# SSM output tables a quarter early, a third table buffer, regrouped gate matmuls and split z tiles in a hybrid FoX/S5/ConvFFN block

## The chip, the cores and the metric

The kernel runs on one core of one Trainium2 chip. The metric is the time of one execution in device microseconds (us); lower is better. Each kernel's time is the median of several runs. The engines are named as the profile names them: PE (TensorE, matrix multiply), DVE (VectorE), ACT (ScalarE), POOL (GpSimd) and SP (SyncE, which only issues DMAs here).

## The reference

One layer of a hybrid encoder block on 1024 tokens of width 1024, with 16 learned meta tokens put in front (1040 positions in all). The part that the change touches is the mixer:

```
xn   = rmsnorm(h)
q, k, v, f_logit, u, gates = split(xn @ w_in)        # 8 heads x 64; u: 512; gates: 2 x 1024
y_a  = forgetting_attention(q, k, v, f_logit) @ w_attn_out
z    = gelu(s5(u))            # 32 groups x 16 channels, 64 complex states per group
zg   = z @ w_glu
y_s  = zg[:, :1024] * sigmoid(zg[:, 1024:])
g    = sigmoid(gates)
h    = h + (g[:, :1024] * y_a + g[:, 1024:] * y_s) @ w_o
```

Behind it come a gated feed-forward block with a causal convolution of width 3, another residual, and a final norm. Nothing there is touched. All values are float32.

## The kernel before, in words

Each float32 operand is split into a high and a low part of 128x128 blocks (`whi`/`wlo` for weights, `xhi`/`xlo` for the normed input), and each product is three matmuls: hi·hi, hi·lo, lo·hi (L159 to L161, called dense below). One gate chunk is 128 gate channels over 1026 columns: three column blocks of 342 (`QBLK`), eight blocks of the depth, three matmuls each, so 72 dense matmuls. There are 16 gate chunks. The eight for the SSM half (i = 8 to 15) and one of the attention half (`AHEAD = 1`, i = 0) run in the gate stage, beside the SSM. The rest run later, as filler between the scores and products of attention (`GA = [1, 1, 1, 3]` chunks per pair of heads).

The program before the feed-forward part goes: load, norm and split of x (to about 60 us) together with the product for u; the gate stage with the SSM (about 60 to 200 us); forget gate, q and k of the first pair of heads; the product of z with `w_glu` (`seven`, L221 to L223, a form with seven half-size products; from 235 us); then attention (first scores, L748 and L749, at 383 us).

The SSM works in chunks of eight positions and in four quarters of eight groups each. Per quarter q:
- input table: DVE makes `Vm`, PE transposes it, ACT copies it to `Wi` (L1756);
- chain, first part: PE multiplies `Wi` with `U`, ACT copies `wr`, `wi` (L1771, L1772);
- output table (`output_tables`): DVE makes `Gm` (products into `Gm` and `tm`, then a difference), PE multiplies it with the input matrix, ACT copies that into `Kt` (L1733), DVE adds a diagonal to `Kt` (16x128), and eight DMAs on SP lay `Kt` out as a block Toeplitz matrix `Tm` (L1741);
- chain, second part: DVE rotates `wr`, `wi` (with cosines and sines made by `rotation`, one for quarters 0 and 1, one for 2 and 3), scans along the chunks, and writes the states `St`;
- chain, third part: PE sums `Gm`·`St` (L1811) and `Tm`·`U` (L1813) into `Y`, ACT copies (L1814) and applies gelu (L1815), a DMA stores `Y` to `y_d`.

`Gm` and `Tm` have two buffers each, `St` and `Y` share three. Before the change the third part of quarter q stands right behind the output table of quarter q, and `rotation(1)` stands inside the second part of quarter 2.

The order on each engine isn't written out: instructions are recorded in a program order, and a scheduler orders each engine's queue by it and by data. On its engine each instruction is then run in that order, and a waiting instruction holds up all behind it. Tiles live in pools; a tile on memory that another held waits until the other's last use. Attention's filler is a generator (`stream`) from which `fill` draws an equal share at each of 28 hooks in a pair.

For z, `load_z` reads `y_d` back into four tiles `zt`, casts them to hi (ACT, L586) and lo (DVE, L129) in `zhi`/`zlo` of four blocks, and forms the differences `zf` (L596 to L599) that become z1, z2, z3 and the block T4 (ACT cast L603, DVE lo L129). The weights' sums and parts are the tiles `ops` (L616).

Of the kernel before, what the change touches and what calls it, by code (L numbers as in the profile page):

```python
# [9 lines left out]
F = mybir.dt.float32  # L10
# [9 lines left out]
P = 128  # L20
# [30 lines left out]
def block_kernel(ctx, tc, x, meta, xbt, x0t, g1t, w_q, w_k, w_v, w_f, w_u, w_g, b_f, w_ao, lam_d, bw_d, cw_d,  # L51
# [7 lines left out]
    def pool(stack, name, bufs=1, side=None, **k):  # L59
        return stack.enter_context(  # L60
            tc.tile_pool(name=name, bufs=bufs, side=side, reuse_waits="tile", **k))
# [216 lines left out]
    xlo = xp.tile([P, KD, L], R, name="xlo")  # L278
    st_s = ExitStack()
    sp = pool(st_s, "ssm", side="left")  # L280
    st_n = ExitStack()
    n1 = pool(st_n, "norm1", side="left")

# [6 lines left out]
    g1T = n1.tile([P, KD], F, name="g1T")  # L290
    S.dma_start(g1T, g1t)
    GP.dma_start(xm, meta)
    ssm_log, ssm_loads, ssm_steps = ssm(tc, after, sp, st_ps, ident, u_d, y_d, lam_d, bw_d, cw_d, d_sk, l_dt)
    queue = []

    def load(dst, src):
# [2 lines left out]
        if len(queue) > 1:  # L299
            after(*queue[:-3:-1])  # L300

    FIRST = [(0, 1), (1, 1), (2, 2), (4, 2), (6, 2)]
    for k, n in FIRST:
        load(xT[0][k // 4][:, k % 4:k % 4 + n], x0t[:, k:k + n])
        load(uraw[k // 2][:, k % 2:k % 2 + n], w_u[:, k:k + n])
# [7 lines left out]

    def load_x(i):
        tag, bufs = ("Gm", 2) if i in (5, 6) else ("sy", 3)
        place[i] = sp.tile([P, D], F, tag=tag, name="xt", bufs=bufs)
        load(place[i], x[P * (i - 1):P * i])

    load_block(1, "Wi")
    for i in range(5, 9):  # L320
        load_x(i)
    us2, ul2 = (sp.tile([P, 2, n, SW if n == 2 else NCH], dt, tag="pc", name=nm, bufs=2)
                for n, dt, nm in ((CH, F, "usb"), (2, R, "ul")))
    ul = [sp.tile([P, 2, SW], R, tag="U", name="ul", bufs=2) for _ in range(2)] + [ul2[:, i] for i in range(2)]


    st_u = ExitStack()
# [85 lines left out]
    for b in (2, 3):  # L413
        last = normed_features(b)
        if b == 2:
            gate0 = [sp.tile([P, KD, P], dt, tag=tag, name="g0", bufs=n)
                     for dt, tag, n in ((F, "Tm", 2), (R, "sy", 3), (R, "Tm", 2))]
            GP.dma_start(gate0[0], w_g[KD])
            S.copy(gate0[1], gate0[0])
            lo_by_dma(gate0[2], gate0[1], w_g[KD])  # L420
        else:
            late.append(last)
        if b == 3:
            for q in (0, 1):
                factors(q)
            for q in (0, 1):
                normed_features(q)
        for m in range(4):
            ps = u_product(b, m)
            S.copy(us_part(b, m), by_chunks(ps[:, :UBLK[b][1]]))  # L430
# [18 lines left out]
        chains[q] = ssm_chain(q)  # L449
        next(chains[q])  # L450

    begin(0)
    ssm_out(0)
    begin(1)
    for q in range(4):
        next(chains[q])
        if q:
            ssm_out(q)
        run(chains[q])
        if q < 2:  # L460
            begin(q + 2)
    st_u.close()
    st_n.close()


    st_f = ExitStack()
    fp = pool(st_f, "fgate", side="right")
    fraw = fp.tile([P, KD, H], F, name="fraw")
# [8 lines left out]
    gp_ = pool(st_g, "gates", side="right")  # L477

    okeep = {}
    AHEAD = 1  # L480

    def gate_chunk(i, pl, tanh):
        whi, wlo = gate0[1:] if i == KD else wchunk(w_g[i], KD, GP, act=not tanh)
        if tanh:
            gs = pl.tile([P, LQ], F, tag="gs", name="gs", bufs=1)
        for t, n in QBLK:
            ps = mm_ps()
            yield from dense_steps(ps[:, :n], whi, wlo, xhi[:, :, T0 + t:T0 + t + n],
                                   xlo[:, :, T0 + t:T0 + t + n], KD)
            if tanh:  # L490
                S.activation(gs[:, t:t + n], ps[:, :n], AF.Tanh, scale=0.5)
            else:
                gs = pl.tile([P, LQ // 3], F, tag="gs", name="gs", bufs=2)
                S.activation(gs, ps[:, :n], AF.Sigmoid)  # L494
                GP.dma_start(g_d[P * i:P * i + P, t:t + n], gs)
        if tanh:
            GP.tensor_scalar(gs, gs, 0.5, 0.5, ALU.mult, ALU.add)
            if pl is not gp_ and i == KD - 1:
                okeep["g"] = gs
            else:  # L500
                SY.dma_start(g_d[P * i:P * i + P], gs)

    for i in [*range(KD, 2 * KD), *range(AHEAD)]:
        run(gate_chunk(i, gp_, False))
    st_g.close()
    st_s.close()

# [54 lines left out]
    TH = L // 2  # L562
    NC2 = NCH // 2
    T3, T2, T1 = ([zp.tile([P, 2, TH], R, name=f"z{i}{w}") for w in "hl"] for i in (3, 2, 1))
    zhi = zp.tile([P, 4, L], R, name="zhi")
    zlo = zp.tile([P, 4, L], R, name="zlo")

    def zblock(r, h_):
        return [t_[:, 2 * r:2 * r + 2, TH * h_:TH * h_ + TH] for t_ in (zhi, zlo)]

    def fold(t_):
        return t_.rearrange("p (n j) -> p j n", j=CH)
# [1 line left out]
    def load_z():  # L574
        zts = []
        for m in range(4):
            tag = "gl" if m % 2 else "ms"
            zt = gz.tile([P, CH, NCH], F, tag=tag, name="zt", bufs=2)
            ym = y_d[m].rearrange("(j c) g n -> g c j n", c=GC)
            for g in range(GQ):  # L580
                (GP if m == 3 and g % 2 else SY).dma_start(zt[GC * g:GC * g + GC], ym[g])
            zts.append(zt)
        for m in range(4):
            w_ = NC2 if m < 2 else NCH
            zh, zl = (fold(t_[:, m, :CH * w_]) for t_ in (zhi, zlo))
            S.copy(zh, zts[m][:, :, :w_])  # L586
            split_lo(V, zl, zts[m][:, :, :w_], zh)

        def part(r, h_, k):
            return zts[2 * r + k][:, :, NC2 * h_:NC2 * h_ + NC2]  # L590

        T4 = zblock(0, 1)
        for k in range(2):
            fa, fb = (gz.tile([P, L], F, tag="cg", name="zf", bufs=2) for _ in range(2))
            f1, f2, f3, f4 = (fold(f_[:, TH * q:TH * q + TH]) for f_ in (fa, fb) for q in range(2))
            V.tensor_tensor(f1, part(0, 1, k), part(0, 0, k), ALU.subtract)  # L596
            GP.tensor_tensor(f3, part(1, 1, k), part(0, 1, k), ALU.subtract)
            V.tensor_tensor(f2, part(1, 1, k), f1, ALU.subtract)
            V.tensor_tensor(f4, part(1, 0, k), f2, ALU.subtract)  # L599
            for f_, t_ in zip((fa, fa, fb, fb), (T1, T2, T3, T4)):  # L600
                q = 0 if t_ is T1 or t_ is T3 else TH
                hi, lo = t_[0][:, k], t_[1][:, k]
                S.copy(hi, f_[:, q:q + TH])  # L603
                split_lo(V, lo, f_[:, q:q + TH], hi)
        return T4

    def glu(i):
# [208 lines left out]
        S.copy(ot[:, :w], po[64:, :w])  # L816
        V.tensor_tensor(ob[64 * e:64 * e + 64, :w], po[:64, :w], ot[:, :w], ALU.add)

    GA = [1, 1, 1, 3]
    SLACK = 5  # L820
    QKN = 2 * len(BLK) * 3 * KD
    GAN = len(QBLK) * 3 * KD
# [33 lines left out]

    units = [((0,), e) for e in range(2)] + [((c, c + 1), e) for c in range(1, len(TILES), 2) for e in range(2)]
    mm_n[1] = False
    done = AHEAD
    for pr in range(H // 2):  # L860
        fbs = []
        for e in range(2):
# [614 lines left out]
        room[0] += len(groups[g])  # L1477


def ssm(tc, after, sp, s_ps, ident, u_d, y_d, lam_d, bw_d, cw_d, d_sk, l_dt):  # L1480
    nc = tc.nc
    V, S, GP, PE, SY = nc.vector, nc.scalar, nc.gpsimd, nc.tensor, nc.sync
    n_small = [0]
# [13 lines left out]
    bufs = dict(Gm=2, Tm=2, Wi=2, U=2, tq=3, sy=3, wr=2, wi=2, dt8=1, ta=1, tb=1, pc=2, dg=1)  # L1497

    def big(tag, shape, name=None):
        return sp.tile(shape, F, tag=tag, name=name or tag, bufs=bufs[tag])  # L1500

    def sm(shape, name=None, dt=F):
        n_small[0] += 1
# [16 lines left out]
    def rest():  # L1520
# [194 lines left out]

            return g0, bcx, bcp

        def output_tables(qt):
            g0, bcx, bcp = views(qt)
            Gm = big("Gm", [P, GQ, CH + 1, GC])  # L1720
            tm = big("tq", [P, GQ, CH + 1, GC], "tm")
            TT(Gm, bcx(cA, CH + 1), bcp(pr, CH + 1), ALU.mult)
            TT(tm, bcx(cB, CH + 1), bcp(pi, CH + 1), ALU.mult)
# [35 lines left out]
        def chain(qt):  # L1759
# [14 lines left out]
            dt8 = big("dt8", [P, HQ, NCH])  # L1774
            S.copy(dt8, dec[:, qt * HQ:qt * HQ + HQ].unsqueeze(2).broadcast_to([P, HQ, NCH]))
            GP.memset(dt8[:, :, 0:1], 0.0)
            if qt == 2:
                rot.append(rotation(1))
            rc, rs = (t_[:, qt % 2 * HQ:qt % 2 * HQ + HQ] for t_ in rot[qt // 2])
            ta, tb = (big(n, [P, HQ, NCH]) for n in ("ta", "tb"))  # L1780
            TT(ta, wr, rc, ALU.mult)
# [34 lines left out]
            GP.dma_start(y_d[qt], Y)  # L1816

        yield input_tables, output_tables, chain

    return log, loads, rest()  # L1820

# [57 lines left out]
```

## Time and profile before

| | |
|---|---|
| time, three runs | 1483.76, 1485.49, 1488.69 us; median 1485.49 us |
| profiled execution | 1486.44 us, span 1484.7 us |
| PE busy | 1440.5 us, 97% of the span |
| DVE, ACT, POOL busy | 73%, 49%, 51% of the span |
| busy PE per 50 us, 150 to 200 us | 46.50 us |
| busy PE per 50 us, 200 to 250 us | 44.07 us |
| busy PE per 50 us, 350 to 400 us | 47.78 us |

The rows of the page give busy time, the share of the span and the number of instructions per engine. A timeline row gives start, duration, engine, line, operation, tiles and sizes; in square brackets stands how long the engine had been idle before it and what it waited for. A windows row gives, for one stretch, its length and the busy time of PE, of PE's weight loads, of DVE, ACT and POOL, then the TensorE clock that was granted (1.00 is full speed), the DMA share and GB/s. Matmuls overlap, so a matmul's duration is longer than its step to the next.

### The profile page before, as it was taken

The page shows a single profiled execution, that of the slowest core. Times are in us where ns is not written, and L with a number is a line of the kernel's source. Part 1 is how long each engine was busy: PE and PEld are TensorE (multiplying, and loading weights), DVE is VectorE, ACT ScalarE, POOL GpSimd, SP SyncE. Part 2 cuts the span into 40 slices and gives each one's busy share as a digit, 9 for nine tenths or more (in the row PEclk, how much of TensorE's full clock was granted, in tenths as well). Part 3 has the DMA queues.
Part 4 walks back from the last instruction along what each step waited for, and adds up shares of the span by engine and source line. Part 5 has one row for each costly group of instructions (what it writes and reads, how often), then busy time and mean ns, then how long its engine had stood idle before and what let it go on. Part 6 is the DMA issues. An engine that isn't in the chain of part 4 may idle for free. (4 is left out here: it accounts for less than half of the span.)

```text
span 1484.7 us, 26535 instructions
## 1 busy us (share of the span) xinstructions
PE 1440.5 (97%) x9646; PEld 1357.2 (91%) x9646; DVE 1079.2 (73%) x2197; ACT 725.6 (49%) x1420; POOL 759.0 (51%) x890
## 2 busy tenths in 40 slices
PE   8999998999999999999999999999999999998997
PEld 7999987998899999999889999999999999777786
DVE  6987929882566676656468977888887766788685
ACT  7545547541465565542645534444434445553433
POOL 1632224752446556513862144555544327789766
PEclk9999998999899999999999999999999999999999
DMA  7665481451117342156974145677653214866413
GB/s 281 188 163 135 128 158 59 158 170 43 41 58 192 94 97 94 37 173 223 267 176 151 58 134 130 176 187 198 173 140 109 80 59 170 293 205 157 140 50 114
DMA packets 89558, 209.85 MB, mean 141 GB/s; under 512 B 14458, under 2 KB 22026, under 8 KB 89044
## 3 DMA queue, kind: packets, MB, share of 16 engines
q1 hardware_dynamic: 69492, 161.50, 32.7%
q0 software_dynamic: 18208, 42.98, 15.0%
q10 hardware_dynamic: 1728, 3.68, 0.7%
q8 instruction: 76, 1.25, 0.3%
q14 instruction: 54, 0.44, 0.1%
HBM read 169.04 MB, written 69.35 MB: 161 GB/s over the span
## 5 line engine op out<-in xcount | busy, mean ns | idle before, releaser
L159 PE MATMUL mm<-xhi,whi 128*128 128x342 f32 (+2 forms) x480 | 157.0, 327 | 0.0
L161 PE MATMUL mm<-xhi,wlo 128*128 128x342 f32 (+2 forms) x480 | 156.6, 326 | 0.0
L160 PE MATMUL mm<-xlo,whi 128*128 128x342 f32 (+2 forms) x480 | 155.6, 325 | 0.0
L1114 POOL TENSOR_TENSOR ov<-ov,og 128x1024 f32<-128x1024 f32 x21 | 51.1, 2435 | 123.4 <-ACT og L1113 119.5
L129 DVE TENSOR_TENSOR sw<-sf,sw 128x512 fp32r<-128x512 f32 x72 | 70.3, 977 | 51.6 <-ACT sw L1105 51.3
L1105 ACT CAST sw<-sf 128x512 fp32r<-128x512 f32 x72 | 45.0, 625 | 106.7 <-POOL sf L1231 74.5
L160 PEld LDWEIGHTS mm<-xlo,whi 128*128 128x128 f32 x480 | 91.1, 190 | 0.6 <-issue 0.4
L159 PEld LDWEIGHTS mm<-xhi,whi 128*128 128x128 f32 x480 | 91.1, 190 | 0.5 <-ACT gs L494 0.2
L161 PEld LDWEIGHTS mm<-xhi,wlo 128*128 128x128 f32 x480 | 91.0, 189 | 0.5 <-issue 0.2
L798 ACT CAST th<-tp 128x256 fp32r<-128x256 f32 (+3 forms) x120 | 56.2, 472 | 63.0 <-PE tp L791 32.1
L1231 POOL TENSOR_TENSOR sf<-raw,sf 128x512 f32<-128x512 f32 x36 | 61.4, 1704 | 44.0 <-DVE sw L129 43.9
L129 DVE TENSOR_TENSOR tl<-tp,th 128x256 fp32r<-128x256 f32 (+3 forms) x120 | 65.2, 546 | 25.0 <-ACT th L798 23.8
L1231 POOL TENSOR_TENSOR sf<-raw 128x512 f32<-128x512 f32 x36 | 47.8, 1328 | 68.9 <-DMA raw<-in_w_up_dram 39.1
L223 PE MATMUL mm<-xhi,sw 128*128 128x258 f32 (+1 forms) x288 | 81.0, 281 | 0.0
L221 PE MATMUL mm<-xhi,sw 128*128 128x258 f32 (+1 forms) x288 | 80.8, 281 | 0.0
L222 PE MATMUL mm<-xlo,sw 128*128 128x258 f32 (+1 forms) x288 | 80.7, 280 | 0.0
L763 POOL TENSOR_SCALAR pt<-pt,nm 128x144 f32<-128x144 f32 (+4 forms) x72 | 52.3, 738 | 51.0 <-DVE nm L762 50.5
L1283 DVE SCALAR_TENSOR_TENSOR ov<-hv,cwt,ov 128x1024 f32<-128x1024 f32 x36 | 73.9, 2054 | 0.2 <-ACT ov L1281 0.2
L1105 ACT CAST sw<-raw 128x512 fp32r<-128x512 f32 x70 | 43.0, 620 | 47.4 <-PE sp L223 19.4
L761 ACT ACTIVATE pt<-pt,nm 128x144 f32<-128x144 f32 (+4 forms) x72 | 53.0, 736 | 25.2 <-DVE nm L760 24.7
L754 DVE CUSTOM_DVE_ANT_0 pt<-sp,fb 128x328 f32<-128x328 f32 (+8 forms) x112 | 46.2, 429 | 21.2 <-PE tp L791 9.8
L129 DVE TENSOR_TENSOR sw<-raw,sw 128x512 fp32r<-128x512 f32 x70 | 56.0, 803 | 5.5 <-ACT sw L1105 4.9
(717 smaller groups left out, 5744.5 us busy)
## 6 DMA issues: line engine op xcount, KB each, us to landing
raw<-in_w_up_dram SPq DMA_DIRECT2D x44, 512.0 KB, 3.7
t_d<-in_w_dn_dram POOLq DMA_DIRECT2D x44, 256.0 KB, 6.7
ar<-a_d SPq DMA_DIRECT2D x44, 256.0 KB, 5.3
wr<-t_d SPq DMA_DIRECT2D x44, 256.0 KB, 2.8
a_d<-ov SPq DMA_DIRECT2D x21, 512.0 KB, 2.6
wr<-in_w_dn_dram SPq DMA_DIRECT2D x33, 256.0 KB, 4.1
t_d<-in_w_dn_dram SPq DMA_DIRECT2D x22, 256.0 KB, 4.3
t_d<-t_d SPq DMA_DIRECT2D x22, 256.0 KB, 4.5
```

The lines of the kernel that those rows point to most:

```text
L129: return eng.tensor_tensor(out_, src, hi.bitcast(F), ALU.subtract)
L159: yield PE.matmul(ps, whi[:, i, :], ahi[:, i], start=(i == 0), stop=False)
L160: yield PE.matmul(ps, whi[:, i, :], alo[:, i], start=False, stop=False)
L161: yield PE.matmul(ps, wlo[:, i, :], ahi[:, i], start=False, stop=(i == k - 1))
L221: PE.matmul(ps, a[0][:, i], bh, start=(i == 0 and not joins), stop=False, skip_group_check=True)
L222: PE.matmul(ps, a[0][:, i], bl, start=False, stop=False, skip_group_check=True)
L223: PE.matmul(ps, a[1][:, i], bh, start=False, stop=(i == kh - 1), skip_group_check=True)
L761: S.activation(pt[:n, :kc], pt[:n, :kc], AF.Exp, bias=nm[:n, 1:2], scale=0.125, accum_out=nm[:n, 2:3])
L798: S.copy(th[:kn, z:tw], tp[:kn, z:tw])
L1105: S.copy(hi, src)
L1231: sums.append(GP.tensor_tensor(f_, a, b, op))
L1283: V.scalar_tensor_tensor(out=o, in0=h_[:, j:SEQ + j], scalar=cwc(j, m), in1=o, op0=ALU.mult, op1=ALU.add)
```

## The change

Seven things are changed.

1. The tiles of the SSM pool are first taken in the order of their lives (`hold`), and the ones for `sy` and `U` go to a pool of their own, `ssmio`.
2. The output table of quarter 2 gets its `Gm` from a third buffer, in a pool `ssmx`.
3. `ssm_out(q + 1)`, the output table of the next quarter, is recorded ahead of the third part of quarter q; the gate matmuls are drawn from a generator, up to 288, 360, 480 and 540 of them ahead of the second part and output of quarters 0 to 3. `rotation(1)` is recorded on its own behind quarter 1's output.
4. The second group of input loads of two blocks becomes two of one.
5. The first gate chunk of the stage (i = 8) takes its column blocks in reverse order.
6. `zhi`/`zlo` of four blocks become two pairs of two blocks; the blocks 0 and 1 are split first, then for each k the differences, then the block 2 + k.
7. The gate chunk i = 0 moves from the gate stage into the filler of the first pair of heads (`GA = [2, 1, 1, 3]`), where it goes through the tanh form of the gate and its weights are split by POOL.

```diff
+    sio = pool(st_s, "ssmio", side="left")
+    for tag, n, cols in (("Gm", 2, 1152), ("Tm", 2, 1024), ("Wi", 2, 1024), ("pc", 2, 2080), ("tq", 3, 1152)):
+        sp.tile([P, cols], F, tag=tag, name="hold", bufs=n)
...
-    FIRST = [(0, 1), (1, 1), (2, 2), (4, 2), (6, 2)]
+    FIRST = [(0, 1), (1, 1), (2, 1), (3, 1), (4, 2), (6, 2)]
...
-    begin(0)
-    ssm_out(0)
-    begin(1)
-    for q in range(4):
-        next(chains[q])
-        if q:
-            ssm_out(q)
-        run(chains[q])
-        if q < 2:
-            begin(q + 2)
...
-        for t, n in QBLK:
+        for t, n in QBLK[::-1] if i == KD else QBLK:
...
-    for i in [*range(KD, 2 * KD), *range(AHEAD)]:
-        run(gate_chunk(i, gp_, False))
+    def stage_gates():
+        for i in range(KD, 2 * KD):
+            yield from gate_chunk(i, gp_, False)
+
+    BEHIND = (288, 360, 480, 540)
+    gates = stage_gates()
+    n_gate = [0]
+
+    def advance(q):
+        while n_gate[0] < BEHIND[q]:
+            next(gates)
+            n_gate[0] += 1
+
+    st_x = ExitStack()
+    sx = pool(st_x, "ssmx", side="left")
+    begin(0)
+    ssm_out(0)
+    begin(1)
+    for q in range(4):
+        next(chains[q])
+        if q < 3:
+            ssm_out(q + 1, sx if q == 1 else None)
+        advance(q)
+        run(chains[q])
+        if q < 2:
+            begin(q + 2)
+        if q == 1:
+            next(ssm_steps)
+    st_x.close()
+    run(gates)
...
-    zhi = zp.tile([P, 4, L], R, name="zhi")
-    zlo = zp.tile([P, 4, L], R, name="zlo")
+    zs = [[zp.tile([P, 2, L], R, name=f"z{w}{r}") for w in "hl"] for r in range(2)]
...
-        for m in range(4):
+        def split_z(m):
             w_ = NC2 if m < 2 else NCH
-            zh, zl = (fold(t_[:, m, :CH * w_]) for t_ in (zhi, zlo))
+            zh, zl = (fold(t_[:, m % 2, :CH * w_]) for t_ in zs[m // 2])
             S.copy(zh, zts[m][:, :, :w_])
             split_lo(V, zl, zts[m][:, :, :w_], zh)
+
+        split_z(0)
+        split_z(1)
...
+            split_z(2 + k)
...
-    GA = [1, 1, 1, 3]
+    GA = [2, 1, 1, 3]
...
-    done = AHEAD
+    done = 0
...
-        def output_tables(qt):
+        def output_tables(qt, pl=None):
...
-            Gm = big("Gm", [P, GQ, CH + 1, GC])
+            Gm = pl.tile([P, GQ, CH + 1, GC], F, name="Gm") if pl else big("Gm", [P, GQ, CH + 1, GC])
...
-            if qt == 2:
-                rot.append(rotation(1))
```

Three places show how this moves instructions. ACT's queue around the end of the third quarter's output (`Y`), before: the two copies of the last `Kt` stand behind the three copies and the gelu of the `Y` of quarter 2.

```order
L1814 COPY Y<-sp 128x390
L1814 COPY Y<-tp 128x390
L1814 COPY Y<-sp 128x260
L1815 ACT_TABLE_LOAD
L1815 ACTIVATE Y<-Y 128x1040
L1733 COPY Kt<-tp 16x512
L1733 COPY Kt<-sp 16x512
L494 ACT_TABLE_LOAD
L494 ACTIVATE gs<-mm 128x342
L146 CAST whi<-raw 128x1024
L494 ACTIVATE gs<-po 128x342
L135 ACTIVATE wlo<-whi 128x1024
```

The same place on ACT's queue now (line numbers of the changed kernel run some 20 higher):

```order
L484 ACTIVATE gs<-mm 128x342
L1754 COPY Kt<-sp 16x512
L1754 COPY Kt<-tp 16x512
L146 CAST whi<-raw 128x1024
L484 ACTIVATE gs<-mm 128x342
L135 ACTIVATE wlo<-whi 128x1024
L1796 COPY dt_2165<-sm_993 128x520
L484 ACTIVATE gs<-mm 128x342
L484 ACTIVATE gs<-po 128x342
L1833 COPY Y<-sp 128x390
L1833 COPY Y<-tp 128x390
L1833 COPY Y<-sp 128x260
```

The copies of the last `Kt` moved ahead of the copies of quarter 2's `Y`, with a gate chunk's work between.

DVE's queue where quarter 2 begins (`rt`, `pc`: the steps of `rotation(1)`; `St` memset: the first touch of quarter 2's states; `Gm<-sm`: the first product of quarter 3's output table), before:

```order
L1491 TENSOR_TENSOR dg<-ident,sm_122 16x128
L1491 TENSOR_TENSOR tm<-sm_120,sm_922 128x1152
L1491 TENSOR_TENSOR Gm<-Gm,tm 128x1152
L1491 TENSOR_TENSOR rt<-pc,sm_981 128x2x8 x2
L1491 TENSOR_TENSOR pc<-rt 128x8 x2
L1491 TENSOR_TENSOR rt<-pc,sm_982 128x2x16 x2
L1491 TENSOR_TENSOR pc<-rt 128x8x2 x2
L1491 TENSOR_TENSOR rt<-pc,sm_982 128x2x32 x2
L1794 MEMSET St 128x8
L1491 TENSOR_TENSOR Gm<-sm_120,sm_922 128x1152
L1491 TENSOR_TENSOR pc<-rt 128x8x4 x2
L1491 TENSOR_TENSOR rt<-pc,sm_982 128x2x64 x2
```

The same stretch of DVE's queue now:

```order
L1512 TENSOR_TENSOR dg<-ident,sm_130 16x128
L1512 TENSOR_TENSOR tm<-sm_128,sm_934 128x1152
L1512 TENSOR_TENSOR rt<-pc,sm_993 128x2x8 x2
L1512 TENSOR_TENSOR Gm<-Gm,tm 128x1152
L1512 TENSOR_TENSOR pc<-rt 128x8 x2
L1813 MEMSET St 128x8
L1512 TENSOR_TENSOR rt<-pc,sm_994 128x2x16 x2
L1512 TENSOR_TENSOR pc<-rt 128x8x2 x2
L1512 TENSOR_TENSOR rt<-pc,sm_994 128x2x32 x2
L1512 TENSOR_TENSOR pc<-rt 128x8x4 x2
```

Quarter 3's first product of `Gm` moved out of this stretch, to a place before quarter 1's states; the rest of `rotation(1)` still stands behind the memset of `St`.

PE's queue at the first scores of attention (`sp<-k,q` and `sp<-kl,qz`: scores; `mm<-xhi,whi` and its like: the dense filler), before:

```order
L748 MATMUL sp<-k_2575,q_2573 128x144
L749 MATMUL sp<-kl,qz_4247 128x144
L748 MATMUL sp<-k_2575,q_2573 128x272
L749 MATMUL sp<-kl,qz_4246 128x272
L748 MATMUL sp<-k_2576,q_2574 128x144
L749 MATMUL sp<-kl,qz_4249 128x144
L791 MATMUL tp<-ident,pt 16x16
```

The same place on PE's queue now:

```order
L160 MATMUL mm<-xlo,whi 128x384
L161 MATMUL mm<-xhi,wlo 128x384
L159 MATMUL mm<-xhi,whi 128x384
L160 MATMUL mm<-xlo,whi 128x384
L161 MATMUL mm<-xhi,wlo 128x384
L159 MATMUL mm<-xhi,whi 128x384
L160 MATMUL mm<-xlo,whi 128x384
L769 MATMUL sp<-k_2503,q_2501 128x272
L770 MATMUL sp<-kl,qz_4174 128x272
L769 MATMUL sp<-k_2504,q_2502 128x144
L770 MATMUL sp<-kl,qz_4177 128x144
L812 MATMUL tp<-ident,pt 16x16 x2
```

Between the first pair of scores of the first head and the first of the second head eight dense matmuls of the filler now stand, where none stood.

## What is forecast

> **What bounds the kernel now.** I read the page first, then busy time by stretches, then PE's waits in each stretch that isn't full, then the timelines there.
>
> ```profile
> PE 1440.5 (97%) x9646; PEld 1357.2 (91%) x9646; DVE 1079.2 (73%) x2197; ACT 725.6 (49%) x1420; POOL 759.0 (51%) x890
> ```
>
> PE is the bound, with 44 us of idle time in 1484.7 of span. Both versions issue the same matmuls, so a gain can come only from these gaps and from the granted clock. The stretches (length; busy PE, PEld, DVE, ACT, POOL; clock; DMA):
>
> ```profile
> 50.00:100.00 50.00, 47.59 (x316) 45.89 (x315) 46.22 (x119) 23.27 (x48) 24.60 (x46) 0.97 0.61 151
> 100.00:150.00 50.00, 48.42 (x345) 47.28 (x345) 39.62 (x67) 29.69 (x53) 12.51 (x22) 1.00 0.59 143
> 150.00:200.00 50.00, 46.50 (x316) 45.16 (x315) 32.47 (x54) 22.23 (x38) 9.30 (x16) 0.97 0.63 142
> 200.00:250.00 50.00, 44.07 (x265) 41.85 (x264) 35.08 (x42) 35.77 (x58) 18.60 (x20) 0.90 0.45 97
> 350.00:400.00 50.00, 47.78 (x224) 39.88 (x223) 14.36 (x69) 13.07 (x35) 7.99 (x28) 0.90 0.07 22
> 400.00:450.00 50.00, 48.84 (x348) 47.46 (x346) 34.81 (x139) 32.01 (x73) 27.60 (x57) 1.00 0.16 51
> ```
>
> Four of them, from 50, 150, 200 and 350, lose PE time and clock together. The waits in them (total, times, longest, us), in order of time:
>
> ```profile
> PE mm L159 <- ACT xhi L366: 2.4, 1, 2.4
> PE tp L1813 <- DMA Tm<-Kt: 1.5, 1, 1.5
> PE tp L1813 <- DMA raw<-in_w_glu_dram: 3.5, 1, 3.5
> PE sp L223 <- DVE ops L129: 2.5, 1, 2.5
> PE mm L221 <- ACT ops L616: 2.0, 1, 2.0
> PE sp L222 <- DVE z2l L129: 1.2, 1, 1.2
> PE sp L748 <- DVE nm L762: 2.1, 1, 2.1
> ```
>
> I call them A (58 us: the first gate chunk waits for the normed x), B and C (141 and 191 us: `Tm` of quarters 1 and 3), D (236 to 246 us: the three waits of the z product) and E (384 us: first softmax of attention). C is put down to a transfer of `w_glu`, but L1813 reads `Tm`, whose DMAs stand just ahead on the same queue. What follows a gap matters too:
>
> ```profile
> 61.00:66.00 5.00, 5.00 (x24) 5.00 (x23) 5.00 (x9) 2.29 (x6) 3.35 (x8) 0.66 1.01 213
> 195.00:199.00 4.00, 4.00 (x22) 4.00 (x22) 0.00 (x0) 0.49 (x2) 0.00 (x0) 0.57 1.13 169
> 235.00:255.00 20.00, 13.56 (x79) 12.35 (x78) 19.03 (x28) 12.50 (x31) 12.09 (x11) 0.74 0.25 79
> 386.00:397.00 11.00, 10.66 (x36) 8.92 (x37) 5.70 (x39) 4.70 (x18) 4.56 (x16) 0.53 0.01 1
> ```
>
> Clock 0.66 over 5 us is 2 x 0.34 x 5 = 3.4 us at half speed; 0.57 over 4 is 3.4 again; 0.74 over 20 and 0.53 over 11 are 10.3 us each. PE was busy nearly throughout after A, C and E, so half speed cost up to 1.7, 1.7 and 5.1 us. After B, 1.45 us long, the clock stayed at 1.00 (the stretch from 100 to 150).
>
> **B and C: output tables a quarter early.**
>
> ```profile
> 131.47 0.28 DVE L1491 TENSOR_TENSOR Kt<-Kt,dg 16x128 f32<-16x128 f32 x1 [1.12 <-ACT Kt L1733]
> 131.83 6.28 SPq L1741 DMA_DIRECT2D Tm<-Kt  x8
> 141.08 0.32 PE L161 MATMUL mm<-xhi,wlo 128*128 128x342 f32 x1
> 142.85 0.46 PE L1813 MATMUL tp<-U,Tm 128*128 128x130 f32 x2 [1.45 <-DMA Tm<-Kt]
> 145.83 1.34 DVE L1491 TENSOR_TENSOR Gm<-sm,sm 128x1152 f32<-128x1152 f32 x1 [8.59 <-issue]
> 171.68 1.42 DVE L1491 TENSOR_TENSOR St<-ta,wr 64x516 f32<-64x516 f32 x2
> 182.81 0.27 DVE L1491 TENSOR_TENSOR Kt<-Kt,dg 16x128 f32<-16x128 f32 x1
> 183.12 1.42 DVE L1491 TENSOR_TENSOR St<-ta,wr 64x516 f32<-64x516 f32 x2
> 189.75 0.32 PE L159 MATMUL mm<-xhi,whi 128*128 128x342 f32 x1
> 191.02 0.31 PE L161 MATMUL mm<-xhi,wlo 128*128 128x342 f32 x1
> 194.83 0.46 PE L1813 MATMUL tp<-U,Tm 128*128 128x130 f32 x2 [3.50 <-DMA raw<-in_w_glu_dram]
> ```
>
> From the end of the diagonal's addition to the first use of `Tm` pass 142.85 - 131.75 = 11.1 us, and 194.83 - 183.08 = 11.75 for quarter 3. Dense matmuls are (191.02 - 189.75) / 8 = 0.16 us apart. In the new order PE has 78 + 45 dense matmuls (19.5 us) and the whole `Y` of quarter 2 (3.8 us at the 0.22 us of these rows) between the product for the last `Kt` and the `Y` of quarter 3: 23 us. ACT's copies and DVE's addition take some 2 to 4 of them, the DMAs 11.75; 7 remain. Quarter 1 gets its table a whole quarter early likewise. So both gaps go: -1.45 and -3.50, and with C its half-speed stretch, -1.7. Together **-6.65**.
>
> That needs DVE, the engine that is next late. Its longest idle in this stage is the 8.59 us ahead of 145.83, in which it waits to touch quarter 2's `St` until PE has finished the `Y` of quarter 1 (ending at 145.8; that row's own `Gm` stands right behind). The new order keeps this wait, but PE is there earlier: counting the rows up to that point, 26 rows fewer (4.1 us) and no B (1.45), so at about 140.2, or 138.5 if A goes too. From there to quarter 2's states DVE took 173.1 - 145.8 = 27.3 us; three table operations of some 1.35 us leave this stretch (they go ahead of the wait), which makes 23.3, and the states stand at 163.5, or 165 with another wait of 1.45 for `Kt`. PE asks for them 26 us (16 dense, one `Wi`, the 8 `Wps`, 38 + 8 + 14 + 78 dense, `Kt`) after that same `Y`, at 166. Quarter 3's states follow 183.12 + 1.42 - 173.1 = 11.4 us later, at 176; PE asks for them at 191.3 - 1.45 - 69 x 0.158 = 179. Margins of 1 to 3 us: thin, and my first rival. I take 0 for it, with 0 to 8 as its bounds.
>
> **A: reversed columns.**
>
> ```profile
> 59.98 1.31 ACT L366 ACTIVATE xhi<-xT,g1T 128x256 fp32r<-128x256 f32 x3
> 64.17 2.07 DVE L367 SCALAR_TENSOR_TENSOR xlo<-xT,g1T,xhi 128x256 fp32r<-128x256 f32 x5
> ```
>
> The last columns are normed first, so the first 24 dense matmuls can start at 58.1 instead of 60.5 and end at 61.9. The next need `xlo` of the block that DVE makes from 64.17 on (0.47 us for the first): 64.7. The gap moves to 62.4 and is some 2.3 us long. PE comes out of it having done the same work, so the gap alone is worth nothing; if the clock is kept, 1.7 us are won, if not, 0. I take half: **-0.8** (bounds -1.7 and +0.5).
>
> **D: z in pairs, and the chunk of 72 moved.** The moved chunk takes 72 x 0.158 = 11.4 us from the gate stage and puts them into the first pair's filler, where PE is busy 48.84 of 50: **0**, and POOL, which splits its weights there, is busy 27.60 of 50. z itself:
>
> ```profile
> 224.14 0.41 ACT L616 CAST ops<-raw 128x256 fp32r<-128x256 f32 x1 [1.96 <-PE mm L160]
> 225.87 6.64 ACT L586 CAST zhi<-zt 128x520 fp32r<-128x520 f32 x4
> 228.97 7.56 DVE L129 TENSOR_TENSOR zlo<-zt,zhi 128x520 fp32r<-128x520 f32 x4
> 240.91 0.80 PE L223 MATMUL sp<-z2h,ops 128*128 128x260 f32 x2 [2.52 <-DVE ops L129]
> 245.61 0.58 PE L221 MATMUL mm<-zhi,ops 128*128 128x260 f32 x1 [2.05 <-ACT ops L616]
> ```
>
> Everything here starts when PE frees the weights of q (ACT's wait at 224.14), and PE needs only the 72 dense matmuls of k from there to the z product, in both versions. DVE is busy 19.03 of the 20 us. The new order does z1 to z3 ahead of the two long blocks, so the wait for `z2l` goes; but the same casts and lo parts still stand ahead of the `ops` that PE waits for at 240.91, and one difference more (`zf`, 1.22 us). So PE gets there about 1.1 us later (18.1 after q's end, was 17.0), and the wait at 245.61 shrinks by as much, since ACT's queue is no shorter. One gap of 5.7 instead of three: **0** (bounds -0.8 and +1.5), half speed kept.
>
> **E: filler at the first scores.**
>
> ```profile
> 381.76 0.34 PE L160 MATMUL mm<-xlo,whi 128*128 128x384 f32 x1
> 382.63 0.34 PE L159 MATMUL mm<-xhi,whi 128*128 128x384 f32 x1
> 383.38 0.34 PE L748 MATMUL sp<-k,q 128*128 128x144 f32 x1
> 386.34 0.46 PE L748 MATMUL sp<-k,q 128*128 128x144 f32 x1 [2.07 <-DVE nm L762]
> ```
>
> The first pair's filler grows from 216 to 288; less the 24 drawn ahead, over 28 hooks, that is 10 a hook instead of 7. The new order has eight dense matmuls between these two rows of scores, where none stood: 8 x (382.63 - 381.76) / 5 = 1.4 us. The gap shrinks from 2.07 to 0.7: -1.4. A gap below B's 1.45 hasn't cost the clock here, so the 10.3 us at half speed should go. PE was full in them, but with 36 matmuls of a stage that waits on softmax, so some of the time would come back as waits: 0 to 5.1, and I take half, -2.6. **-4.0** together.
>
> [...]
>
> Layout, third buffer and the split of the loads of the start (two short transfers where one stood): **0**, since PE has no waits at 62 to 141 us but those named, with 0.5 either way.
>
> **Sum.** -6.65 - 0.8 - 4.0 = -11.45 on the profiled execution's 1486.44 us: **1475.0**. That execution lies 0.95 above the median of 1485.49, within the runs' 1483.76 to 1488.69. Within 0.3% (4.5 us) of the median I call no change, which is about what a measurement of this kernel can tell.
>
> **Rivals.**
> 1. DVE is late for quarters 2 and 3. For it: the margins of 1 to 3 us, and a DVE that was busy 46.22 of the 50 us from 50 on. Two gaps of A's 2.4 us, each with 1.7 of half speed, are 8.2: 1483. Chance 0.18.
> 2. Slower: the chain of DVE stalls as it did, once more in full. Each `Kt` addition now stands on DVE ahead of an earlier quarter's states, and waits for PE and ACT; what waits behind it are the scans. If the 8.59 us come again behind the new `Kt`, quarter 3's states come at 184.5 + 8.6 = 193, and PE, at 179, waits 14 us and pays up to 5.1 for the clock: 1475 + 19 = 1494. It decides from a stall of some 11 us, where the sum is spent. Against it: PE's `Kt` products stand 23 us and more ahead of their quarter's `Y`. Chance 0.11.
> [...]
> 4. The moved tables do nothing, because `Tm` is held by something else (its DMAs queue behind others on SP): only E and A remain, 1481.7. Chance 0.07, within 0.3% or just above.
>
> **Chances and range.** The forecast (1470 to 1478) holds 0.5. Faster: 0.5, with rival 3's 0.14, and half of rivals 1 and 4, 0.12: 0.76. Same: the other half, 0.12. Slower: rival 2 and 0.01 for what I don't see, 0.12. The low end takes every lower bound: A -1.7, E -7.2, D -0.8, and B and C -6.65: 1470, less 1 for the other small waits of the first pair. The high end takes rival 1 with D's +1.5, and 1 for the runs: 1486.
>
> **What would show it.** Right: no PE wait at L1813 (now L1832), DVE's longest idle of the SSM stage well below 8.59, z's product starting some 19 us earlier (11.4 + 6.65 + 0.8), clock 1.00 behind the first scores, one wait of 5 to 6 us in z's product. Wrong: PE waits for `St` at quarter 2 or 3; a clock of 0.5 for 10 us at the first scores; a second gap in z's product; PE waiting for `whi` or `wlo` in the first pair.

## The result and the profile after

The changed kernel takes 1477.23 us in the median of 13 runs (1472.85 to 1483.98); the kernel before, measured with it, 1483.77 us (13 runs, 1481.0 to 1488.69). The ratio is 0.9954 with a 95% interval of 0.9939 to 0.9968: 0.46% faster, some 6.8 us. The forecast was 1475.0, 0.7% under the median it was made against. The direction is right and the size is about two thirds of the forecast. The way there is not the one forecast.

The profiled execution after took 1479.76 us, 6.7 less than the one before. Its page:

```profile
span 1478.0 us, 26529 instructions
PE 1432.5 (97%) x9646; PEld 1351.2 (91%) x9646; DVE 1075.8 (73%) x2198; ACT 724.0 (49%) x1419; POOL 770.1 (52%) x888
```

PE is still 97% busy, and its idle time is 45.5 us, a little more than before. What fell is its busy time, by 8 us. Most of that can be the clock: up to 400 us PE ran at half speed (a granted clock of 0.50: 63 to 65 and 387 to 396 us before, 78 to 80 us after) for some 14 us of this execution where it had been some 27, by the sum used in the forecast. Half of the difference, up to 7 us, is what that is worth. The four stretches that lost PE time and clock, after (length; busy PE, PEld, DVE, ACT, POOL; clock; DMA):

```profile
50.00:100.00 50.00, 42.80 (x281) 41.05 (x280) 42.82 (x105) 20.48 (x40) 23.00 (x41) 0.97 0.63 147
150.00:200.00 50.00, 49.67 (x348) 47.63 (x347) 28.18 (x46) 23.84 (x37) 12.27 (x20) 1.00 0.65 152
200.00:250.00 50.00, 39.95 (x256) 39.17 (x257) 43.52 (x63) 36.35 (x68) 26.62 (x23) 0.90 0.20 62
350.00:400.00 50.00, 47.79 (x287) 42.92 (x286) 24.34 (x115) 21.71 (x57) 16.97 (x46) 1.00 0.11 36
```

Two stretches got better: 150 to 200 us (the last tables) and 350 to 400 us (the first scores, clock 1.00 where it was 0.90). Two got worse: 50 to 100 us lost nearly 5 us more of PE's time, 200 to 250 us 4 us more. (The stretches are fixed in time, and the work in them has moved: the z product now starts 14 us earlier.) PE's waits from 50 to 400 us with a longest piece of 0.6 us or more, in order of time, show what stands there now:

```profile
PE mm L160 <- DVE xlo L370: 2.5, 1, 2.5
PE mm L159 <- ACT gs L484: 2.9, 1, 2.9
PE sp L1789 <- ACT Wi L1777: 1.7, 1, 1.7
PE mm L159 <- DVE fl__2342 L533: 1.7, 1, 1.7
PE sp L223 <- DVE ops L129: 6.0, 1, 6.0
PE mm L221 <- ACT c L230: 2.5, 1, 2.5
PE sp L769 <- DVE mx L775: 0.9, 2, 0.6
```

No wait at the product with `Tm` is left: B and C are gone. In their place stand three that weren't there: 2.9 us at 73 us for the store tile of the first gate block, 1.7 us at 86.5 us for `Wi`, 1.7 us at 199.7 us for the forget gate. The wait of 2.9 us was also followed by half speed, 0.72 over 6 us and 0.50 from 78 to 80:

```profile
76.00:82.00 6.00, 5.75 (x27) 5.75 (x28) 6.00 (x15) 0.54 (x2) 1.26 (x4) 0.72 0.81 246
```

Stages of the two profiled executions, from the start times of PE's rows (u done: the end of its last matmul; z product: first matmul with `ops`; feed-forward: first matmul with `sw`):

| stage | before, us | after, us | difference | less the moved chunk (11.4) |
|---|---|---|---|---|
| start to u done | 58.13 | 55.40 | -2.7 | -2.7 |
| u done to z product (gate stage) | 177.48 | 166.03 | -11.45 | 0.0 |
| z product to feed-forward (with attention) | 560.52 | 567.44 | +6.9 | -4.5 |
| feed-forward to end | 688.6 | 689.1 | +0.6 | +0.6 |

How much a single execution can say: the last row, which no edit here touches, lies between 686.4 and 690.6 us in the profiled executions of the fourteen kernels of this document, so differences of 2 us between two traces need the medians beside them.

In these two executions the gate stage got shorter by the moved chunk and by nothing else. Its waits before, with half speed at half the time it lasted: A 2.41 + 1.7, B 1.45, C 3.50 + 1.7, together 10.8 us. After: 2.55, 2.93 + 1.7, 1.72, 1.70 and 0.17, together 10.8. All that the tables won there stands again as other waits in the same stage. What stayed in this execution is the start and attention.

The three new waits each have a place in the trace. At 73 us, ACT and DVE of the changed kernel:

```profile
74.44 1.28 ACT L484 ACT_TABLE_LOAD   x1 [8.46 <-DMA u_d<-usb]
74.52 1.36 DVE L1512 TENSOR_TENSOR Gm<-sm,sm 128x1152 f32<-128x1152 f32 x1 [3.52 <-DMA u_d<-usb]
```

By this wait, the tile into which ACT puts the first finished gate block (the store tile) lies on memory of `usb`, and has to wait until the stores of u from there have landed. That wait was there before too (7.07 us of ACT), but PE came late enough not to meet it. The third table's buffer, by its wait, lies there as well: DVE, which makes the rest of the SSM's set-up in order, stands 3.5 us behind the first product of quarter 2's table, a product that isn't needed until much later. The wait for `Wi` at 86.5 us comes after both: the two `Wi` copies of ACT stand behind a gate weight's cast, which waits for PE.

At 199.7 us, POOL and ACT of the changed kernel:

```profile
188.84 0.54 POOL L485 DMA_DIRECT2D g_d<-gs  x1 [1.23 <-ACT gs L484]
192.75 2.13 POOL L598 DMA_DIRECT2D zt<-y_d  x4 [3.36 <-issue]
194.87 0.57 POOL L485 DMA_DIRECT2D g_d<-gs  x1
```

```profile
200.42 1.12 ACT L532 COPY fx<-mm 8x272 f32<-8x272 f32 x3 [9.05 <-DMA g_d<-gs]
```

POOL issues the last gate store behind four loads of z that have to wait for the stored `Y` of quarter 3: that store is issued at 187.07 us and takes 5.1 us to land, and POOL stands 3.36 us ahead of the loads. The forget gate's tile `fx`, by its wait, lies on the memory of that store's source, so ACT waits 9 us for it, DVE behind ACT, PE behind DVE, and the z product's casts behind them.

### The profile page after: what moved, and what is told of

It reads as the page before. It is cut to its first block, busy times and chain, and to the rows that moved or that the text cites. A ratio compares the mean times of both kernels' runs of the same rounds, so it can differ in the third digit from the quotient of the medians.

```text
span 1478.0 us, 26529 instructions
## 1 busy us (share of the span) xinstructions
PE 1432.5 (97%) x9646; PEld 1351.2 (91%) x9646; DVE 1075.8 (73%) x2198; ACT 724.0 (49%) x1419; POOL 770.1 (52%) x888
## 5 line engine op out<-in xcount | busy, mean ns | idle before, releaser
L129 DVE TENSOR_TENSOR sw<-sf,sw 128x512 fp32r<-128x512 f32 x72 | 66.7, 927 | 50.4 <-ACT sw L1126 50.2
```

The lines of the kernel that those rows point to most:

```text
L129: return eng.tensor_tensor(out_, src, hi.bitcast(F), ALU.subtract)
```

## The experiments

Theory W at first was: the tables win what B and C cost, and the moved chunk takes the cover from other waits, so that it costs the gate stage about what it wins in attention. Its rivals: the gain is the start and the filler (S), or the tables carry it (T); later, that the stage is set by a chain through the stores of u and through DVE, so that the tables only move waits (Q). Each ratio is to runs of the kernel before that were taken with it.

| kernel | what it is | ratio | 95% interval |
|---|---|---|---|
| changed | | 0.9954 | 0.9939 to 0.9968 |
| first_only | before + loads of the start | 0.9987 | 0.9973 to 1.0000 |
| chunk_only | before + moved chunk | 0.9977 | 0.9961 to 0.9992 |
| tables_only | before + tables, third buffer, layout | 0.9987 | 0.9974 to 0.9999 |
| no_first | changed, loads as before | 0.9957 | 0.9944 to 0.9969 |
| no_chunk | changed, chunk back in the stage | 0.9947 | 0.9927 to 0.9968 |
| tables_old | changed, tables as before | 0.9937 | 0.9919 to 0.9955 |
| z_at_once | changed, z split at once | 0.9946 | 0.9925 to 0.9966 |
| no_rev | changed, columns in order | 0.9924 | 0.9910 to 0.9937 |
| third_late | changed, third table later on DVE | 0.9933 | 0.9914 to 0.9953 |
| three | changed, three waits taken away or cut short | 0.9957 | 0.9941 to 0.9972 |
| late_chunk_back | third_late and no_chunk | 0.9949 | 0.9937 to 0.9962 |
| late_chunk_back_z | the same and z_at_once | 0.9957 | 0.9942 to 0.9972 |

### first_only and no_first: the loads of the start

```diff
-    FIRST = [(0, 1), (1, 1), (2, 2), (4, 2), (6, 2)]
+    FIRST = [(0, 1), (1, 1), (2, 1), (3, 1), (4, 2), (6, 2)]
```

(first_only: this in the kernel before; no_first: the reverse in the changed one.)

> The kernel before with one edit: the split of the second load of two blocks at the start. Theory S (the start and the filler carry the gain; the gate stage gives back what the tables win): the product for u ends about 2.7 us earlier (55.4 instead of 58.1 us), but the gate stage meets its stores and waits a little earlier, so 0 to 2.7 us of it stay: 1481 to 1484. Rival T (the tables carry the gain, the earlier start is the clock's phase): u ends within 1 us of before and the time doesn't change, 1483.8 within 1.

> The changed kernel with the loads of the start as before. Theory S: u ends at about 58 us again; the wait for the first gate store's memory at 73 us (2.9 us) shrinks to under 1, since PE comes there later, so that of the 2.7 us half or less is lost: 1477 to 1480. Rival T: the same time as the changed kernel, 1477 within 1, with u at 55 to 56 us.

first_only ends u at 56.3 us and takes 0.9987 of before, some 2 us, with an interval that reaches 1.0000. no_first ends u at 58.3 us and yet takes the same time as the changed kernel, as theory S has it. Rival T put the earlier start down to the clock; the granted clock was 1.00 from 0 to 58 us before and from 0 to 56 us after, so in these two it isn't that. Its waits in the gate stage say where the start's gain goes:

```profile
PE mm L160 <- DVE xlo L370: 2.4, 1, 2.4
PE sp L1789 <- ACT Wi L1777: 1.7, 1, 1.7
PE mm L159 <- DVE fl__2338 L533: 0.9, 1, 0.9
PE mm L159 <- ACT gs L484: 0.6, 1, 0.6
```

The wait for the store tile is 0.6 us instead of 2.9, since PE comes 2.9 us later to a tile that is free when the stores of u have landed. The edit that I had costed at nothing moves the end of u by 2 to 3 us between these executions, and the changed gate stage gives it back. The end of u varies on its own, too: with the loads as before it lies between 56.1 and 58.3 us in four profiled executions, with the split loads between 54.6 and 57.6 in ten; the means are 57.4 and 55.5. What the start loses can be seen on SP's queue and on PE, before:

```profile
4.01 2.15 SPq L298 DMA_DIRECT2D uraw<-in_w_u_dram  x1
6.21 0.74 SPq L298 DMA_DIRECT2D xa<-in_x0t_dram  x1
```

```profile
8.13 0.43 PE L336 MATMUL po<-xhi,ul 128*128 128x272 f32 x1
10.19 0.60 PE L334 MATMUL mm<-xhi,uh 128*128 128x272 f32 x1 [1.63 <-ACT uh L392]
```

The load at 4.01 us is that of blocks 4 and 5 of u's weights, two blocks in one. After, it stands at 5.36 us, behind the one more pair of loads, and takes 0.67 us to issue, and PE has no wait there. But tables_only, with the loads as before, takes 1.10 us for it and PE waits 0.29 us, so the unsplit loads don't always show it, and why the issue takes so long stays open.

### no_chunk and chunk_only: the moved gate chunk

```diff
-            for i in range(KD, 2 * KD):
+            for i in [*range(KD, 2 * KD), 0]:
...
-    GA = [2, 1, 1, 3]
+    GA = [1, 1, 1, 3]
...
-    done = 0
+    done = 1
```

(no_chunk, from the changed kernel; chunk_only sets `AHEAD = 0` and `GA = [2, 1, 1, 3]` in the kernel before.)

> The changed kernel with the gate chunk back in the gate stage (and 1 chunk in the first pair). Theory S: the half-speed stretch of 10 us and the wait of 2 us at the first scores come back: 5 to 6 us slower than the changed kernel, about 1482.5; against it the last gate store no longer holds up the forget gate (1.7 us), so 1481 to 1483. Rival T: the place of the chunk is neutral, 1477 within 1.

> The kernel before with the gate chunk moved into the first pair of heads and nothing else. Theory W: the first scores keep full clock (5 to 6 us won), and the waits for Tm of quarter 3, the forget gate and the z product grow by about as much: 1482 to 1488, no change. Rival S: 5 to 6 us faster than before, 1478 to 1480.

The filler does what was forecast: in chunk_only PE's waits for the first scores are 0.9 us in two pieces, and the clock there is full (1.00); in no_chunk 1.7 us is back in one piece, with 6.8 us at half speed. But no_chunk isn't slower. Waits that the changed kernel has in its gate stage and z product are shorter or gone with the chunk back as cover. The five longest from 60 to 400 us that are left:

```profile
PE sp L223 <- DVE ops L129: 3.9, 1, 3.9
PE mm L160 <- DVE xlo L370: 2.6, 1, 2.6
PE sp L769 <- DVE mx L775: 1.9, 2, 1.7
PE mm L221 <- ACT ops L637: 1.8, 1, 1.8
PE sp L1789 <- ACT Wi L1777: 1.7, 1, 1.7
```

The z product waits 5.7 us instead of 8.5, the store tile 0.2 instead of 2.9, and the forget gate doesn't wait at all; new is a wait of 1.2 us for U. chunk_only, 3.4 us faster than before (interval 0.9961 to 0.9992), shows the price in the old order: the wait for z's low part is 3.6 us there where it was 1.2. Its 1482.71 us lie in theory W's range. So rival T's number came out (the chunk is neutral in the changed kernel: 1478.04 us against 1477.23) and theory W's reason for it.

### tables_old and tables_only: the tables alone, and all but them

```diff
-        if q < 3:
-            ssm_out(q + 1, sx if q == 1 else None)
-        advance(q)
+        if q:
+            ssm_out(q)
         run(chains[q])
```

(tables_old, from the changed kernel. tables_only is the changed kernel with no_first's, no_chunk's, no_rev's and z_at_once's edits together.)

> The changed kernel with the output tables recorded as before (each in its own quarter, two buffers, all gate matmuls behind). Theory W (the tables win some 6.6 us at quarters 1 and 3, and the moved chunk costs the gate stage and the z product about what it wins in attention): the waits for Tm come back, 1.5 and 3.5 us with 1.7 for the clock or more, since a chunk of cover less stands ahead of them: 1484 to 1490. Rival S (the gain is attention's filler, the gate stage nets nothing): within 1.5 us of the changed kernel, 1476 to 1479.

> The kernel before with the tables a quarter early, the third buffer and the layout alone: start loads, columns, z and the chunk as before (z in two pairs of tiles, all split at once). Theory P (the gap's price holds where its cover stands: with the chunk in the stage, the tables win what their waits cost): the waits at 141 and 191 us go with the clock behind them, some of it returns as DVE's stall on the third buffer: 4 to 7 us faster than before, 0.995 to 0.997. Rival Q (the stage is set by the chain of the SSM through DVE and the stores of u, so the tables move waits only): within 2 us of before.

Both W and P (the tables win what their waits cost) fall here, and the numbers are those of their rivals: 1476.93 us for tables_old lies in S's range, and tables_only, 1483.38 us, within Q's 2 us of before. Without the early tables the changed kernel is as fast as with them: 0.9937 against 0.9954, intervals overlapping. Alone on the kernel before they win 0.1%, hardly more than nothing. The waits did go: tables_only has none at `Tm`. What PE waits for in its gate stage from 100 us on is the u of quarter 2:

```profile
PE tp L1788 <- DMA U<-u_d: 2.0, 1, 2.0
```

and half speed follows it for 3.4 us, so 3.7 us of the 6.65 are gone again there. In tables_old the wait for `Tm` of quarter 3 is back with 2.1 us and 3.4 us of half speed, 3.8 in all instead of 5.2 before, and quarter 1's isn't there. The 6.65 us were a true reading of two waits in one execution, and not what the tables are worth. (tables_old keeps the new layout and the early `rotation(1)`; these weren't tried alone.)

### no_rev: the order of the columns

```diff
-        for t, n in QBLK[::-1] if i == KD else QBLK:
+        for t, n in QBLK:
```

> The changed kernel with the first gate chunk's columns in order, as before. As forecast (the gap only moves, and the clock is kept about every second time instead of never): the wait of 2.4 us stands at 55.4 us ahead of the chunk again, half speed follows in the profile, and the median is 0 to 2 us above the changed kernel's ratio, 0.995 to 0.997. If the order of the columns decides what PE does at 73 us (it comes there 1.7 us later): no difference, since the wait there shrinks by as much.

The opposite of the forecast: without the reversed columns the changed kernel takes 1474.26 us (5 runs, 1471.79 to 1475.21), the fastest here, and its interval ends just below the changed kernel's. In the profiled executions the clock at the first wait isn't the reason: the wait did only move, and half speed, which was expected behind it in no_rev, didn't come; the clock from 57 to 72 us was 1.00, as in the changed kernel. Over all profiled executions the clock was kept more often with the reversal: from 60 to 72 us it was 1.00 in four of nine with reversed columns, and half speed followed the first wait in four of five with the columns in order. So the half of 1.7 us was read about rightly. What the reversal changes besides is, among other things, the order of POOL's queue, 130 us later. Without it:

```profile
189.99 0.54 POOL L1835 DMA_DIRECT2D y_d<-Y  x1 [6.57 <-ACT Y L1834]
192.69 0.54 POOL L485 DMA_DIRECT2D g_d<-gs  x1 [2.17 <-ACT gs L484]
193.65 0.89 POOL L136 DMA_DIRECT2D wlo<-in_w_k_dram  x1 [0.41 <-ACT wlo L135]
194.24 2.48 POOL L598 DMA_DIRECT2D zt<-y_d  x4
```

```profile
195.79 0.75 ACT L532 COPY fx<-mm 8x272 f32<-8x272 f32 x2 [2.45 <-DMA g_d<-gs]
```

The last gate store stands ahead of the loads of z, ACT waits 2.45 us for it instead of 9.05, the wait at the forget gate is gone, and the z product waits 3.6 and 2.5 us instead of 6.0 and 2.5. That is 1.7 + 2.4 = 4.1 us, against 3 us between the medians; of the 6.0 us between the two spans 1.35 lie in the gate stage, where 2.5 us of waits for U are new, and 3.0 from the z product to the feed-forward part. That the swap of the store and the loads is the cause is not shown, and `three`, below, speaks against it: it makes the same swap, with two other edits, and wins nothing. What makes no_rev faster stays open.

### z_at_once: the split of z

```diff
-        split_z(0)
-        split_z(1)
+        for m in range(4):
+            split_z(m)
...
-            split_z(2 + k)
```

> The changed kernel with all four blocks of z split ahead of the differences, as before, still in two pairs of tiles. If the order of the splits is worth nothing (as forecast): the three waits of the z product come back as 1.2, 2.5 and 2.0 us instead of 6.0 and 2.5, which sums to 2 to 3 us less: 1475 to 1477. If the split was worth what it was written for: the waits sum to more than 8.5 us, and the time is 1478 or above.

0.9946, 1476.9 us: no difference that can be told from the changed kernel. The three waits of the z product in its profile are back, with 2.5, 3.5 and 0.9 us instead of 6.0 and 2.5; the forecast of nothing for this order held.

### third_late, three, late_chunk_back and late_chunk_back_z: taking the new waits away

```diff
             TT(Gm, bcx(cA, CH + 1), bcp(pr, CH + 1), ALU.mult)
+            if pl:
+                after(log[-1], kt_add[-1])
...
             TT(Kt[:, :, :GC], Kt[:, :, :GC], dg, ALU.add)
+            kt_add.append(log[-1])
```

(third_late. `three` adds the two edits below; late_chunk_back adds no_chunk's edit to third_late, late_chunk_back_z z_at_once's too.)

```diff
-            ps = mm_ps()
+            ps = st_ps() if i == KD + 1 and t else mm_ps()
...
-                (GP if m == 3 and g % 2 else SY).dma_start(zt[GC * g:GC * g + GC], ym[g])
+                ld = (GP if m == 3 and g % 2 else SY).dma_start(zt[GC * g:GC * g + GC], ym[g])
+                if m == 3 and g % 2:
+                    after(ld, stores[-1])
```

> The changed kernel with the first product of the third table ordered behind quarter 1's Kt addition on DVE, so that it no longer waits for the stored u with the set-up of the SSM behind it. Theory W: the idle time of DVE at 71 to 74.5 us (3.5 us) goes, Vm of quarter 0 comes that much earlier, and the wait of 1.7 us for Wi at 86.5 us shrinks; the first gate store's wait stays: 0 to 2 us faster than the changed kernel, 1475 to 1477. If DVE has slack there: no change, 1477 within 1.

> The changed kernel with third_late's edit, the loads of z on POOL ordered behind the last gate store, and two blocks of the second gate chunk in PSUM banks of the other pool, so that PE has six blocks instead of four until the first gate store. Theory W: the waits at 73 us (2.9, with 1.7 of clock), 86.5 us (1.7) and 199.7 us (1.7) go or shrink below 1: 4 to 7 us faster than the changed kernel, 1470 to 1473. Rival: the z product starts earlier by that, but waits longer, since its own chain (stored y, loaded z, casts) doesn't start earlier: 1475 to 1477.

> The changed kernel with the third table's product late and the gate chunk back in the stage. If the waits are separate: third_late's gain and no_chunk's add, 0.991 to 0.993 of before. If they stand for the same time (one wait takes over from the other): 0.993 to 0.996, as each alone.

> The same with all four blocks of z split at once. If z's order is worth nothing: the same ratio within 0.0015. If the split in two steps costs what z_at_once's waits in the profile say (6.4 against 8.5 us): 1 to 2 us faster than late_chunk_back.

In third_late DVE's wait of 3.5 us for the stored u is gone and PE's wait for `Wi` falls from 1.7 to 0.6 us, as expected. Its time of 1475.93 us lies in the range given; by the ratio, 0.9933, it is 3 us below the changed kernel, with overlapping intervals, so a gain isn't shown. The first wait of its z product has grown to 7.1 us. `three` takes away the wait for the forget gate, leaves 0.7 us of the one for the store tile and 1.3 us for `Wi`, and wins nothing. Its waits at the z product:

```profile
PE sp L223 <- DVE ops L129: 6.2, 1, 6.2
PE sp L221 <- ACT ops L640: 2.1, 1, 2.1
PE mm L221 <- DVE kl L129: 1.6, 2, 1.4
```

9.9 us instead of 8.7, and 1.0 us for U on the way. The mechanism is that of its rival; the time, 1480.01 us, lies above the rival's 1477, with a ratio equal to the changed kernel's (0.9957). Why the z product isn't ready earlier shows on ACT and DVE of `three`:

```profile
194.15 0.38 ACT L533 COPY fx<-mm 8x272 f32<-8x272 f32 x1 [3.14 <-DMA g_d<-gs]
200.78 2.36 DVE L621 TENSOR_TENSOR zf<-zt,zf 128x520 f32<-128x520 f32 x1 [3.32 <-DMA zt<-y_d]
227.41 0.77 DVE L129 TENSOR_TENSOR ops<-sf,ops 128x256 fp32r<-128x256 f32 x2
```

ACT waits 3.14 us for the gate store instead of 9.05. But then DVE stands 3.32 us at a difference of z, for loads that haven't landed, and the forget gate's next step (`fx`) is behind that in its queue: it starts at 203.0 us, against 203.5 in the changed kernel. The `ops` that PE waits for follow at 227.4, against 228.0. In no_rev that step of the forget gate starts at 198.3 us, ahead of that difference, and the `ops` at 223.9.

late_chunk_back, 0.9949, is no faster than third_late or no_chunk alone: the waits take over from each other instead of adding up. In its profile the store tile's wait is 2.5 us again, and the z product waits 3.6 and 1.8 us. late_chunk_back_z, 0.9957, is within 0.0015 of it, as it should be if z's order is worth nothing.

## Why the prediction was right or wrong

**B and C, -6.65: the waits right, the worth wrong.** The waits went, and DVE kept ahead of PE as worked out: quarter 2's states stood at 167.2 us and PE asked for them at 169.6, quarter 3's at 178.5 and 180.3; margins of 2.4 and 1.8 us where I had 1 to 3. DVE's longest idle of the SSM stage fell from 8.59 to 3.6 us. Rivals 1 and 2 didn't come. Rival 4 had the tables do nothing; they nearly did, though not for its reason, since `Tm` was in time. The step that took 6.65 us off the sum is the one that failed: it put down the waits' length as time won, with nothing behind them. Alone, the tables are worth 0.0013 of the time (0.0001 to 0.0026), 2 us; in the changed kernel, nothing that shows. I asked what was late next only on DVE's path to the states, not on the others that PE meets in the stage. One of the signs named for being right shows it: the z product was to start some 19 us earlier and started 14.2 us earlier, of which 11.4 are the moved chunk and 2.7 the start, and nothing is left for the tables.

**The third buffer, 0: wrong.** It lies on the memory of u, and its first product, early in DVE's queue, waits 3.5 us for u's stores with the SSM's set-up behind it. What that costs in time isn't shown: third_late, without that wait, isn't told apart from the changed kernel.

**A, -0.8: wrong in sign.** The gap moved to 59.6 us and is 2.55 us long (forecast 62.4 and 2.3), and the clock was kept in four of nine profiled executions, near the half that was taken. But in the changed kernel the reversal costs some 3 us in the median, and no term had that. By what, stays open; `three` speaks against the swap on POOL's queue alone.

**The start, 0 within 0.5: wrong.** u is done some 2 us earlier in the mean; alone that wins some 2 us (0 to 4), with the rest nothing that shows.

**The moved chunk, 0: right as a sum, wrong in its parts.** I named attention's filler as its new cover, and didn't price what it had covered before. Without it the forget gate, the store tile and the z product wait.

**D, 0: half right.** The casts go as worked out and the first wait is one of 6.0 us (forecast 5.7). The second gap was named as a sign of being wrong, and it came: the wait that should have shrunk from 2.05 us is 2.5 us, so D is 8.5 us instead of 5.7 in this execution; half speed stayed (granted clock 0.71 from 222 to 236 us).

**E, -4.0: the mechanism right, the size too small in this execution.** The first scores wait 0.6 us (forecast 0.7), and the clock is 1.00 from 350 to 400 us. Attention's stage is 4.5 us shorter with D's 2.8 inside, so E won near 7 us here. No run shows rival 3 (0.14 of the chances), by which the clock at E wouldn't come back: chunk_only has the full clock at the first scores too, with 0.9 us of waits in two pieces, and no_chunk, with a wait of 1.7 us there, has 6.8 us of half speed.

So it is luck that the total lay in the range. A gain some three times too large at the tables stood against gains at the start and in attention that were set too low, and the kernel gives back in one wait much of what it wins in another. Between these kernels the three parts tried alone sum to 0.13 + 0.23 + 0.13 = 0.49%, near the 0.46% of the whole, while taking any one of them out of the whole costs nothing that can be measured. What binds them then isn't settled. A chain through u's stores, the SSM's quarters on DVE and ACT and the stored y into the z product would explain it; it is read from the waits, and no experiment shortened it on its own. Nor is it shown how much of each ratio comes from the scheduler, which orders the queues anew after every edit, as the swap in no_rev shows.

The fastest kernel measured is no_rev, the changed kernel without the reversed columns: 0.9924 of before.

## What to carry to other kernels

In this kernel a wait on the bound engine was worth its length only where nothing else ended just behind it (at B and C 6.65 us of waits and clock were counted, and alone the tables won some 2 us). So before its microseconds go into a sum, follow the next rows of that engine and ask what each would wait for if it came that much earlier, above all for tiles on memory that another transfer still holds. A chunk of work that moves is costed at both ends, as filler where it goes and as cover where it was. And where a scheduler orders the queues, compare the order of every queue, those of the DMAs too, to the end of the stage: here an edit of one chunk's columns swapped a store and four loads on POOL 130 us later. Then try the suspected swap by itself before it is called the cause.

## What the runs showed of the hardware that was not expected

Gaps of nearly the same length, in nearly the same place, were followed by half speed in some executions and not in others. In the nine profiled executions with reversed columns the first wait lasts 2.39 to 2.60 us and ends between 61.4 and 65.0 us; the granted clock from 60 to 72 us was 1.00 in four of them and 0.86 in five. They are of nine kernels, one execution each, but two are alike up to there: in the changed kernel the wait is 2.55 us and ends at 62.18 us, in no_chunk it is 2.60 us and ends at 62.17 us. Their rows, the changed kernel first:

```profile
60.00:72.00 12.00, 9.82 (x62) 9.82 (x63) 10.95 (x49) 1.20 (x3) 7.81 (x15) 1.00 0.98 199
```

```profile
60.00:72.00 12.00, 9.82 (x52) 9.72 (x53) 10.94 (x49) 1.13 (x3) 6.77 (x13) 0.86 0.99 198
```

0.86 over 12 us is 2 x 0.14 x 12 = 3.4 us at half speed again: it followed the gap of 2.60 us in no_chunk and didn't follow the one of 2.55 us in the changed kernel. What decides it, no run here shows.
